# A decoder trunk on one Trainium2 core: down products in pairs of 256 columns, with their weights in two long places

## The chip, the cores and the metric

The kernel runs on one core of a Trainium2 chip. The engines are PE (TensorE, matmuls), PEld (its weight loads), ACT (ScalarE), DVE (VectorE), POOL (GpSimd) and SP (which issues DMAs). The metric is device time of one execution in microseconds (us), lower is better; "before" and "after" are two programs that compute the same.

## The reference

Two layers, each an FFN, a token mixer (differential attention in the first layer, a pooling mixer in the second), cross-attention into 256 memory tokens and another FFN, over 512 tokens of width 1024. What the change touches is the FFN, which runs four times:

```python
def swiglu_ffn(x, w_in, w_out):
    h = x @ w_in
    g, u = jnp.split(h, 2, axis=-1)
    return (jax.nn.silu(g) * u) @ w_out
...
x = layer_norm(a * x + 0.5 * swiglu_ffn(x, ffn_w_in[i, 0], ffn_w_out[i, 0]),
               ln_g[i, 0], ln_b[i, 0])
...
x = layer_norm(a * x + h, ln_g[i, 1], ln_b[i, 1])
x = layer_norm(a * x + memory_cross_attention(x, mem, xa_wq[i], xa_wkv[i], xa_wo[i]),
               ln_g[i, 2], ln_b[i, 2])
x = layer_norm(a * x + 0.5 * swiglu_ffn(x, ffn_w_in[i, 1], ffn_w_out[i, 1]),
               ln_g[i, 3], ln_b[i, 3])
```

`w_in` is 1024 x 5632, `w_out` 2816 x 1024, all in float32.

## The kernel before

**Split operands.** Each float32 operand is kept as two tiles: hi, a cast that ACT makes (`split`, or L746 in `up`), and lo, what the cast lost, a subtraction on DVE (L144, L748). `mm3` (L225) makes a product of two such operands with three matmuls, hi by hi (L231), hi by lo (L232) and lo by hi (L233).

**The FFN.** It is made of blocks of 256 hidden columns, 11 of them. `up` computes gate and value of one block and needs 7 products in place of 8, from sums of quarter matrices; each product is 24 matmuls of 256 columns, with a quarter of `w_in` as the stationary operand (`wh`, `wl`) and x or a sum of its quarters as the moving one (`xh`, `xl`, `xe`). The quarters come as `ra` and `rc`, loaded by SP and added to by POOL's accumulating DMAs (L737, L741). `down` multiplies a pair of blocks by `w_out` with 7 products too; from one split weight each makes 12 matmuls of 512 columns: for two halves of the rows (b = 0, 1) and two hidden blocks (k = 0, 1), three each. Here the hidden block (`ha`, `hb`, from `seven`) is stationary and the split weight (`wh`, `wl`) moves. The raw weights `b1` to `b4` are added to between products (L919), and the sums in PSUM are added to the tokens `X` by DVE (L935). The last three blocks go through `plain_down`, with sums `ps`.

**The order.** `FFN_TURNS` gives five turns: three ups; then two ups and a down (pairs 0 and 1), and so on, so there are four downs in an FFN. The loop of `ffn` steps through the turn's generators ("lanes") in turn, one product each: up, up, down. PE runs the matmuls in that order. ACT and DVE run what the steps issue in an order that the scheduler derives from the same order.

**Places.** A split operand of a stage comes from `hl`, which rotates over four slots of `wh` and four of `wl` (`ffn_pools`, the 4 of `stage_pools`). Pads (`to_w`, `to_x`) set where pools begin: with `APART` of 64 bytes, `ROUND` of 512 and `LINE` of 480, w tiles of an FFN lie at addresses that leave 32 when divided by 512, and x tiles (`xh`, `xl`, `xe`) at addresses that leave 480, 64 bytes below. A matmul of an up thus has its moving operand at 480 and the stationary one that follows at 32; one of a down has its moving operand at 32 like a w, and `ha` or `hb` at 480 like an x. `_x` among the bufs of `ffn_phase` is such a pad.

Of the kernel before, what the change touches and what calls it, by code (L numbers as in the profile page):

```python
# [10 lines left out]
F32R = mybir.dt.float32r  # L11
# [6 lines left out]
P = 128  # L18
D = 1024
S = 512  # L20
# [26 lines left out]
    turn=(1.0, 1.0, 1.2, 1.5),  # L47
# [21 lines left out]
APART, ROUND, LINE = {"ffn": 64, "da": 448, "pool": 64}, 512, 480  # L69
# [47 lines left out]
def drain(units):  # L117
    for _ in units:
        pass


def few(units, n):
    for _ in range(n):
        next(units, None)


class Trunk:
# [147 lines left out]
        if gate == 1:  # L275
            self.queue_behind(self.passes[2], low)

    def hl(self, shape):
        return (
            self.stage["wh"].tile(shape, F32R, tag="wh", name="wh", bufs=self.w_bufs),  # L280
            self.stage["wl"].tile(shape, F32R, tag="wl", name="wl", bufs=self.w_bufs),
        )

    def cols(self, raw, j):

        w = self.hl([P, 8, P])
        self.split_weights(w[0], w[1], raw[:, :, j * P : (j + 1) * P])
        return w
# [281 lines left out]
    def ffn(self, layer, j, ln, beside=()):  # L570
        w_in, w_out = self.a["ffn_w_in"][layer, j], self.a["ffn_w_out"][layer, j]
        self.seven_of, self.factors = {}, self.factor_tiles()
        nc, n, beside = self.nc, len(FFN_TURNS), iter(beside)
        at_start = bool(self.load_rest)
        downs = {i: self.down(d, w_out, 2.0 * ALPHA if i == 1 else 1.0) for i, (_, d) in enumerate(FFN_TURNS) if d}

        def start(turn):
            ups = FFN_TURNS[turn][0]

            early = (2, 1, 1) if turn == 0 else (0, 0)  # L580
            rest = self.load_rest.pop if turn == 0 and at_start else lambda: lambda: None
            got = [self.up(w_in, u, lane, early[lane], rest() if lane == 0 else None) for lane, u in enumerate(ups)]
            for lane, g in enumerate(got):
                next(g)
                if lane == 1:
                    rest()()
            if turn > 1:
                next(downs[turn])
            return got + [downs[i] for i in downs if i == turn]

        works = start(0)
        if at_start:

            zeros = self.act("hb", (P, P + S), mybir.dt.bfloat16)
            nc.vector.memset(zeros, 0.0)
            idle = self.aux("idle", "yz")
            self.warm(zeros, idle, 7)
            for tag, half in (("px", 0), ("py", 1)):
                for t in self.late[:2]:
                    self.turn(t, half, tag)  # L600
                if half == 0:
                    with self.tc.issue_after(self.last_turn.ins):
                        self.warm(zeros, idle, 9)
                next(works[0])
                if half == 0:
                    next(works[0])
            next(works[1])
        else:
            for w in works + works[:1]:
                next(w)  # L610
            self.turn_late(2)
        self.late = []
        next(works[0])
        act, dve = self.first_split
        if self.begins:

            for late, first in zip(self.begins, (act, dve)):
                self.queue_behind(late, first)
        second = self.second_factors()
        if at_start:  # L620

            next(works[0])
            for w in (works[1], second, second, works[1], works[2], works[2], works[0]):
                with self.behind():
                    next(w)
        else:
            for w in (second, *works[1:], second, downs[1]):
                next(w)
        for turn in range(n):
            behind = turn == n - 1  # L630
            for step in range(1 if turn == 0 else 0, 9 if behind else 7):
                if turn == 0 and (step == 3 or step == 2 and at_start):
                    next(second)
                if step == 4:
                    if behind:
                        coming = [self.plain_down(w_out, layer, j, ln, beside)]
                    else:
                        coming = start(turn + 1)
                        if at_start and turn == 0:
                            with self.tc.issue_after(self.last_load.ins):  # L640
                                next(downs[1])
                if behind and step in (4, 6, 7, 8):
                    next(coming[0])
                if behind and step > 3:
                    few(beside, 2)

                for lane, w in enumerate(works[: None if not behind or step > 1 else -1]):
                    if not (at_start and turn == 0 and lane < 2 and step == 1):
                        next(w, None)
                    if turn == 0 and lane == 1 and step == 2 and at_start:  # L650
                        next(works[0])
                    if turn == 0 and lane == 0 and step == 2 and not at_start:
                        next(second)
                    if at_start and turn == 0 and lane == 0 and step == 3:
                        next(works[2])
                if turn == 1 and step == 3:
                    self.seven_of[self.waiting[0]] = self.seven(self.waiting[1])
            works = coming
        drain(works[0])
# [236 lines left out]
    def down(self, pairs, w, scale):  # L896
# [14 lines left out]
        hs = [self.seven_of[u] for u in pairs]  # L911

        def operand(raw):
            t = self.hl([P, 2, S])
            self.split(t[0], t[1], raw)
            return [(t[0][:, i], t[1][:, i]) for i in range(2)]

# [3 lines left out]
        def product(ps, b, a, ws, start=False):  # L921

            o = slice(b * P, (b + 1) * P)
            for k in range(2):
                h, l = hs[k][a]
                self.mm3(ps, (h[:, o], l[:, o]), ws[k], start and k == 0, k == 1, not start)

        started = set()

# [6 lines left out]

        B = range(2)
        ws = operand(b11)
        more(b11, b12)
        xs = []  # L940
        for b in B:
            xs.append(self.aux("px", "px"))
            product(xs[b], b, 0, ws, True)
            add(xs[b], b, 0)
        yield
        ws = operand(b21)
        for b in B:
            ps = self.aux("py", "py")
            product(ps, b, 1, ws, True)
            add(ps, b, 0)  # L950
        yield
        ws = operand(b11)
        more(b11, b22)
        more(b12, b22)
        zs = []
        for b in B:
            zs.append(self.aux("pz", "py"))
            product(zs[b], b, 3, ws, True)
            add(zs[b], 2 + b, 1)
        yield  # L960
        ws = operand(b22)
# [4 lines left out]
        ws = operand(b11)  # L966
# [5 lines left out]
        ws = operand(b12)  # L972
# [4 lines left out]
        ws = operand(b11)  # L977
# [5 lines left out]
    def plain_down(self, w, layer, j, ln, beside):  # L983
# [8 lines left out]
        ws = [[], []]  # L992

        def operand(half, k):
            t = tiles[half][k]
            if half == 0:
                v = self.hl([P, 2, S])
            elif k < 2:
                v = self.pair("hb", (P, 2, S))
            else:  # L1000
                v = [[self.act("ha") for c in range(2)] for _ in range(2)]
                for c in range(2):
                    self.split(v[0][c], v[1][c], t[:, c])
                ws[half].append(v)
                return
            self.second = self.split(v[0], v[1], t)[1]
            ws[half].append([[x[:, c] for c in range(2)] for x in v])

        def product(ps, half, t, k, n=slice(0, S)):
            o = slice(t * P, (t + 1) * P)  # L1010
            for c in range(2):
                h = [x[:, c, o] for x in self.seven_of[FFN_LAST[k]]]
                self.mm3(ps, h, [x[c][:, n] for x in ws[half][k]], k == c == 0, k == 2 and c == 1)

        operand(0, 0)
        yield

        sums = []
        for n, (half, t) in enumerate(LAST):
# [14 lines left out]
            ps = self.aux("ps", ("yz", "py")[n % 2])  # L1034
# [691 lines left out]

    def ffn_pools(self):
        self.apart = APART["ffn"]
        return self.stage_pools(4, dict(ra=4, rc=3), ("wh", "wl", "ra", "rc"))

    def other_pools(self, order=("wh", "wl", "raw"), raw=2):
        return self.stage_pools(5, dict(raw=raw), order)

    def ffn_phase(self, **more):
        bufs = dict(b1=1, b3=1, b2=1, b4=1, _x=0, xe=6, hb=4, sp=4, ha=4, sr=1, hr=3)
        return self.phase_pool(("hr", "sr"), "sp", **bufs, **more)

    def ffn_first(self, layer, ln):
        with self.ffn_pools():
# [83 lines left out]
```

## Time and profile before

| | us |
|---|---|
| median of three runs | 1898.41 (1897.36 to 1905.37) |
| profiled execution | 1899.25 |
| its span | 1897.5 |
| PE idle for a semaphore, all waits | 3.3 |

Rows of the trace read: start in us, duration, engine, line, operation, output from inputs by the program's names, shapes, and in brackets the idle time before it and what ended it. Grouped rows end in the count, the busy time, and the mean of one in ns. Matmuls are pipelined: their durations overlap, and what one costs is the distance from its start to the next start.

### The profile page before, as it was taken

What the parts mean: (1) busy time and instruction counts of PE and PEld (TensorE: products, weight loads), DVE (VectorE), ACT (ScalarE), POOL (GpSimd) and SP (SyncE); (2) the same over time, 40 slices, a digit from 0 to 9 for tenths busy, and PEclk for the clock granted to TensorE, in tenths of its full rate; (3) what the DMA queues carried; (4) which work ended last, traced back from release to release, by engine and by line L of the source; (5) the groups of instructions that cost most, each with busy time, mean ns of one, the idle gap of its engine ahead of it and who ended that gap; (6) DMA issues with size and microseconds to landing.
All of it is one profiled execution on the core that took longest, in us unless ns stands there. A gap on an engine that the chain in (4) does not pass through costs nothing.

```text
span 1897.5 us, 32589 instructions
## 1 busy us (share of the span) xinstructions
PE 1886.5 (99%) x13120; PEld 1730.9 (91%) x13120; DVE 1540.9 (81%) x2246; ACT 1000.8 (53%) x1542; POOL 308.2 (16%) x274
## 2 busy tenths in 40 slices
PE   9999999999999999999999999999999999999998
PEld 8999998888889988999998999999899889999996
DVE  7888989888876558889887988898786568998886
ACT  6555554566654435555554655555455436555552
POOL 3112120112110002221220311212120012211210
PEclk9999999999999999999999999999999999999999
DMA  9978772322235327987785687777464438867861
GB/s 254 215 178 178 171 141 85 103 69 75 91 112 178 112 70 181 195 177 168 144 188 168 118 179 181 168 166 162 157 172 146 142 69 180 173 159 178 185 129 53
DMA packets 250055, 283.20 MB, mean 149 GB/s; under 512 B 8752, under 2 KB 213040, under 8 KB 249904
## 3 DMA queue, kind: packets, MB, share of 16 engines
q0 software_dynamic: 94080, 94.38, 32.3%
q1 hardware_dynamic: 155824, 186.74, 30.2%
q8 instruction: 103, 1.69, 0.4%
q14 instruction: 48, 0.39, 0.1%
HBM read 274.79 MB, written 4.19 MB: 147 GB/s over the span
## 4 chain that ended last, share of the span: by engine, by line
PE 96%; DMA 2%; DVE 1%; ACT 0%; SPq 0%; issue 0%; POOL 0%; DVEq 0%; ACTq 0%
PE x L231 7%; PE x L232 7%; PE x L233 7%; PE ps L231 5%; PE ps L233 4%; PE ps L232 4%; PE z L231 4%; PE z L233 4%; PE z L232 4%; PE px L233 3%; PE px L231 3%; PE px L232 3%; PE x L773 3%; PE y L231 2%; PE y L232 2%; PE y L233 2%
## 5 line engine op out<-in xcount | busy, mean ns | idle before, releaser
L741 POOL DMA_DIRECT2D ra<-in_ffn_w_in_dram x132 | 170.7, 1307 | 977.6 <-DVE wl L748 960.4
L746 ACT CAST wh<-ra 128x1024 fp32r<-128x1024 f32 x176 | 184.9, 1053 | 197.8 <-PE x L232 63.8
L748 DVE TENSOR_TENSOR wl<-ra,wh 128x1024 fp32r<-128x1024 f32 x176 | 214.2, 1220 | 64.7 <-ACT wh L746 64.0
L231 PE MATMUL x<-xe,wh 128*128 128x256 f32 x704 | 195.0, 277 | 0.0
L232 PE MATMUL x<-xe,wh 128*128 128x256 f32 x704 | 194.8, 277 | 0.0
L233 PE MATMUL x<-xe,wl 128*128 128x256 f32 x704 | 194.8, 277 | 0.0
L746 ACT CAST wh<-rc 128x1024 fp32r<-128x1024 f32 x132 | 138.9, 1053 | 100.3 <-PE x L232 41.6
L143 ACT CAST wh<-b 128x1024 fp32r<-128x1024 f32 x112 | 117.8, 1052 | 134.8 <-PE x L232 62.2
L748 DVE TENSOR_TENSOR wl<-rc,wh 128x1024 fp32r<-128x1024 f32 x132 | 159.5, 1218 | 24.7 <-ACT wh L746 24.7
L144 DVE TENSOR_TENSOR wl<-b,wh 128x1024 fp32r<-128x1024 f32 x112 | 136.7, 1220 | 40.9 <-ACT wh L143 40.9
L231 PE MATMUL x<-xh,wh 128*128 128x256 f32 x536 | 148.7, 277 | 0.0
L232 PE MATMUL x<-xl,wh 128*128 128x256 f32 x536 | 148.4, 277 | 0.0
L233 PE MATMUL x<-xh,wl 128*128 128x256 f32 x536 | 148.4, 277 | 0.0
L231 PEld LDWEIGHTS x<-xe,wh 128*128 128x128 f32 x704 | 132.4, 188 | 1.3
L232 PEld LDWEIGHTS x<-xe,wh 128*128 128x128 f32 x704 | 132.3, 188 | 1.3
L233 PEld LDWEIGHTS x<-xe,wl 128*128 128x128 f32 x704 | 132.2, 188 | 0.0
L144 DVE TENSOR_TENSOR wl<-raw,wh 128x1024 fp32r<-128x1024 f32 x64 | 78.5, 1233 | 45.8 <-ACT wh L143 45.2
L231 PEld LDWEIGHTS x<-xh,wh 128*128 128x128 f32 x536 | 100.8, 188 | 0.7
L232 PEld LDWEIGHTS x<-xl,wh 128*128 128x128 f32 x536 | 100.8, 188 | 0.7
L233 PEld LDWEIGHTS x<-xh,wl 128*128 128x128 f32 x536 | 100.7, 188 | 0.0
L143 ACT CAST wh<-raw 128x1024 fp32r<-128x1024 f32 x64 | 66.4, 1049 | 62.5 <-PE xq L232 18.2
L231 PE MATMUL z<-xe,wh 128*128 128x256 f32 x352 | 97.5, 277 | 0.0
(445 smaller groups left out, 6239.9 us busy)
## 6 DMA issues: line engine op xcount, KB each, us to landing
ra<-in_ffn_w_in_dram POOLq DMA_DIRECT2D x132, 512.0 KB, 7.0
rc<-in_ffn_w_in_dram SPq DMA_DIRECT2D x88, 512.0 KB, 5.8
b<-in_ffn_w_out_dram SPq DMA_DIRECT2D x76, 512.0 KB, 5.0
ra<-in_ffn_w_in_dram SPq DMA_DIRECT2D x44, 512.0 KB, 4.7
rc<-in_ffn_w_in_dram POOLq DMA_DIRECT2D x44, 512.0 KB, 7.3
raw<-in_xa_wkv_dram SPq DMA_DIRECT2D x16, 1024.0 KB, 5.4
raw<-in_da_w_qkv_dram SPq DMA_DIRECT2D x24, 512.0 KB, 3.7
raw<-in_xa_wq_dram SPq DMA_DIRECT2D x8, 1024.0 KB, 5.2
```

What stands on the lines that cost most here:

```text
L143: self.nc.scalar.copy(hi, src),
L144: self.nc.vector.tensor_sub(lo, src, hi.bitcast(F32)),
L231: self.first_mm = mm(out, w[0], x[0], start=start, stop=False, skip_group_check=again)
L232: mm(out, w[0], x[1], start=False, stop=False, skip_group_check=again)
L233: self.last_mm = mm(out, w[1], x[0], start=False, stop=stop, skip_group_check=again)
L741: nc.gpsimd.dma_start(t, source(*block), accum_op=ALU.add)
L746: hi = nc.scalar.copy(v[0], raw)
L748: lo = nc.vector.tensor_sub(v[1], raw, v[0].bitcast(F32))
L773: self.last_mm = nc.tensor.matmul(ps[:, j], v[i][:, k, j * P : (j + 1) * P], x[l][:, k], start=n == i == l == 0, stop=n == 7 and i == 1, s ...
```

## The change

`down` now computes each half's product in two parts of 256 columns: for columns 0 to 255 and then 256 to 511, the same 12 matmuls, so a product that was 12 matmuls of 512 columns is 24 of 256. Its split weights come no longer from `hl` but alternate between two long places, `above` (beside `wh` and `wl`, in the stage's pools) and `below` (among the phase's tiles, in place of the pad). A long place holds hi and lo behind each other, and has room for an offset, which puts the operand where x tiles lie (480) or where w tiles lie (32). For the downs it is as x, while `ha` and `hb` move to where w tiles lie, since the pad before them is gone.

`wh` and `wl` have two slots each instead of four. In turn 0, and in step 0 of turn 1, `hl` rotates by fours: two operands to the long places, two to `wh` and `wl`. Five operands get the place of what they meet, by the flag `alike`: one of turn 0, step 4, in each of the four FFNs, and one of a down in turn 1, step 2, of the first. `plain_down` uses the long places as x and gives `hb` an offset; its step at turn 4, step 6 comes behind the second lane instead of ahead of the lanes. The gains of the layer norm are kept in `hr` twice, instead of `hr` and `sr`.

```diff
-    def hl(self, shape):
+    def hl(self, shape, down=None):
+        if down is None and "below" in self.bufs:
+            self.slot += self.by_fours
+            if self.by_fours and self.slot % 4 < 2:
+                alike, self.alike = self.alike, False
+                return self.long_place(self.slot % 2, shape, alike)
...
+    def long_place(self, below, shape, as_x):
+        n, near, far = 2 * S, self.apart // 4, (ROUND - self.apart) // 4
+        if below:
+            t, at = self.act("below", (P, 2 * n + near)), 0 if as_x else near
+        else:
+            t = self.stage["above"].tile([P, 2 * n + far], F32R, tag="above", name="above", bufs=1)
+            at = far if as_x else 0
+        return tuple(t[:, at + i : at + i + n].rearrange("p (a b) -> p a b", a=shape[1]) for i in (0, n))
...
+        self.slot, self.by_fours, self.alike = 0, True, False
...
-                if behind and step in (4, 6, 7, 8):
+                if behind and step in (4, 7, 8):
                     next(coming[0])
...
+                self.by_fours = turn == 0 or turn == 1 and step == 0
+                self.alike = turn == 0 and step == 4 or at_start and turn == 1 and step == 2
                 for lane, w in enumerate(works[: None if not behind or step > 1 else -1]):
...
+                    if behind and step == 6 and lane == 1:
+                        next(coming[0])
...
         def operand(raw):
-            t = self.hl([P, 2, S])
+            self.slot += 1
+            t = self.long_place(self.slot % 2, (P, 2, S), not self.alike)
...
-            for k in range(2):
-                h, l = hs[k][a]
-                self.mm3(ps, (h[:, o], l[:, o]), ws[k], start and k == 0, k == 1, not start)
+            for c, e in ((0, 2 * P), (2 * P, S)):
+                for k in range(2):
+                    h, l = hs[k][a]
+                    self.mm3(
+                        ps[:, c:e], (h[:, o], l[:, o]), [w[:, c:e] for w in ws[k]],
+                        start and c == k == 0, k == 1 and e == S, True,
+                    )
...
             if half == 0:
-                v = self.hl([P, 2, S])
+                self.slot += 1
+                v = self.long_place(self.slot % 2, (P, 2, S), True) if k else self.hl([P, 2, S], True)
             elif k < 2:
-                v = self.pair("hb", (P, 2, S))
+                far = (ROUND - self.apart) // 4
+                v = [t[:, far : far + 2 * S].rearrange("p (a b) -> p a b", a=2) for t in self.pair("hb", (P, far + 2 * S))]
...
-        return self.stage_pools(4, dict(ra=4, rc=3), ("wh", "wl", "ra", "rc"))
+        return self.stage_pools(2, dict(ra=4, rc=3), ("wh", "wl", "above", "ra", "rc"))
...
-        bufs = dict(b1=1, b3=1, b2=1, b4=1, _x=0, xe=6, hb=4, sp=4, ha=4, sr=1, hr=3)
-        return self.phase_pool(("hr", "sr"), "sp", **bufs, **more)
+        bufs = dict(b1=1, b3=1, b2=1, b4=1, sr=1, xe=6, below=1, hb=4, sp=4, ha=4, hr=3)
+        return self.phase_pool(("hr", "hr"), "sp", **bufs, **more)
```

How the order of the instructions moves is shown at three places, each of before (line numbers of before) and then of after (its own line numbers). The first is PE at the first down product of the first FFN; `px` is its sum in PSUM, `ha` the hidden block, `x` and `y` sums of the ups beside it. Before, its 12 matmuls end like this:

```order
L233 MATMUL x<-xh,wl 128x256
L231 MATMUL px<-wh,ha 128x512
L232 MATMUL px<-wl,ha 128x512
L233 MATMUL px<-wh,ha 128x512
L231 MATMUL px<-wh,ha 128x512
```

After, the same place:

```order
L233 MATMUL x<-xh,wl 128x256
L231 MATMUL px<-above,ha 128x256
L232 MATMUL px<-above,ha 128x256
L233 MATMUL px<-above,ha 128x256
L231 MATMUL px<-above,ha 128x256
```

Four such groups of three stood there, and eight stand there now, with half the columns and hi and lo both in `above`.

The second is DVE in the first FFN, where the fourth turn begins, around the adds of its down's first product to the tokens (`X_76`, `X_77`, by `px`) and the subtraction that makes the lo part of that down's second operand (from `b`, into `wl` before and a long place after). Before:

```order
L935 SCALAR_TENSOR_TENSOR X_76<-X_76,px 128x512
L888 TENSOR_TENSOR sr<-hr 128x256
L891 TENSOR_TENSOR sr<-hr 128x256
L889 SCALAR_TENSOR_TENSOR sr<-sr,hr 128x256
L935 SCALAR_TENSOR_TENSOR X_77<-X_77,px 128x512
L890 SCALAR_TENSOR_TENSOR sr<-sr,hr 128x256
L824 TENSOR_TENSOR hr<-y,sp 128x2x256
L144 TENSOR_TENSOR wl<-b_1957,wh 128x1024
L748 TENSOR_TENSOR wl<-ra,wh 128x1024
```

After:

```order
L144 TENSOR_TENSOR below<-b_2069,below 128x1024
L912 SCALAR_TENSOR_TENSOR sr<-sr,hr 128x256
L144 TENSOR_TENSOR hb<-hr,hb 128x256
L770 TENSOR_TENSOR wl<-rc,wh 128x1024
L144 TENSOR_TENSOR hb<-sr,hb 128x1024
L962 SCALAR_TENSOR_TENSOR X_76<-X_76,px 128x512
L910 TENSOR_TENSOR sr<-hr 128x256
L913 TENSOR_TENSOR sr<-hr 128x256
L911 SCALAR_TENSOR_TENSOR sr<-sr,hr 128x256
L962 SCALAR_TENSOR_TENSOR X_77<-X_77,px 128x512
```

The subtraction for that operand (`b_1957` before, `b_2069` after) stood behind the two adds to `X` by `px`, and stands ahead of them now.

The third is ACT at the end of cross-attention and the start of the second FFN. `oT` is attention's output, `p` and `var` belong to the layer norm, `xh` is the normed x, turned (`pt`) and cast, and `ra` and `rc` are quarters of `w_in`. Before:

```order
L143 CAST oT<-xo 128x512 x3
L746 CAST wh<-ra 128x1024 x3
L397 ACTIVATE p,var<-X_76,mean 128x1024
L746 CAST wh<-rc 128x1024
L398 ACTIVATE var<-var 128x1
L397 ACTIVATE p,var<-X_77,mean 128x1024
L398 ACTIVATE var<-var 128x1
L143 CAST xh<-pt 128x4x128 x2
L397 ACTIVATE p,var<-X_78,mean 128x1024
L143 CAST xh<-pt 128x4x128
```

After:

```order
L143 CAST oT<-xo 128x512 x3
L768 CAST above<-rc 128x1024
L768 CAST wh<-ra 128x1024 x2
L414 ACTIVATE p,var<-X_76,mean 128x1024
L415 ACTIVATE var<-var 128x1
L414 ACTIVATE p,var<-X_77,mean 128x1024
L415 ACTIVATE var<-var 128x1
L143 CAST xh<-pt 128x4x128 x2
L414 ACTIVATE p,var<-X_78,mean 128x1024
L143 CAST xh<-pt 128x4x128
L415 ACTIVATE var<-var 128x1
L143 CAST xh<-pt 128x4x128
```

Three casts of `ra` and one of `rc` stood ahead of the first cast of `xh`. Now one of `rc` and two of `ra` do, and the next row behind the last one shown is `CAST below<-ra`, the first operand that PE needs in this FFN. On PE the first product of the FFN used to be 24 matmuls of that one operand, and then `pt` for the third quarter of the tokens; now 16 of them, 15 of another lane's product and the other 8 come ahead of that `pt`.

## The prediction

> **What bounds the kernel now.** I read the page first: the busy shares, the granted clock in 40 slices, and the chain that ended last.
>
> ```profile
> PE 1886.5 (99%) x13120; PEld 1730.9 (91%) x13120; DVE 1540.9 (81%) x2246; ACT 1000.8 (53%) x1542; POOL 308.2 (16%) x274
> ...
> PEclk9999999999999999999999999999999999999999
> ...
> PE 96%; DMA 2%; DVE 1%; ACT 0%; SPq 0%; issue 0%; POOL 0%; DVEq 0%; ACTq 0%
> ```
>
> TensorE is busy for 99% of the span, it is 96% of the last chain, and its clock is full in every slice. So time can only come from two places: gaps on PE, or the start-to-start time of a matmul. The waits of PE (line waited for and releaser; total us, times, longest us) show how little the gaps hold:
>
> ```profile
> PE idle L138 <- DVE hb L595: 1.3, 1, 1.3
> PE ps L231 <- DVE X L380: 0.8, 1, 0.8
> PE y L773 <- ACT wh L746: 0.5, 1, 0.5
> PE xq L233 <- DVE wl L144: 0.3, 1, 0.3
> PE po L1247 <- DVE a L144: 0.2, 1, 0.2
> PE pt L515 <- DVE X L403: 0.2, 1, 0.2
> ```
>
> 3.3 us in all. What is left is the time of one matmul, and that has to be read from starts: the durations in the rows (0.28 us for 256 columns) overlap, since matmuls are pipelined. Next the timeline of PE around one down product, and the windows (length; busy time and count by engine; clock; DMA share; GB/s) of three stretches without a wait:
>
> ```profile
> 109.73 0.39 PE L231 MATMUL px<-wh,hb 128*128 128x512 f32 x1
> ...
> 112.48 0.28 PE L231 MATMUL x<-xe,wh 128*128 128x256 f32 x1
> ...
> 117.94 0.39 PE L231 MATMUL px<-wh,hb 128*128 128x512 f32 x1
> ```
>
> ```profile
> 34.54:76.83 42.29, 42.29 (x361) 42.29 (x360) 33.24 (x39) 24.37 (x31) 10.31 (x8) 1.00 1.16 250
> 745.31:799.60 54.29, 54.29 (x482) 54.29 (x480) 47.30 (x54) 34.63 (x45) 14.21 (x11) 1.00 0.92 175
> 109.73:241.14 131.41, 131.41 (x962) 123.55 (x961) 115.00 (x144) 69.45 (x83) 21.91 (x18) 1.00 0.74 171
> ```
>
> The counts include two or three matmuls that only overlap an edge; what starts inside is 359, 479 and 960. The second window is a turn with only 256-column matmuls: 54.29/479 = **113.3 ns** each. The third holds 16 cycles of one down product (12 matmuls of 512 columns) and two up products (48 of 256): 131.41/16 = 8.213 us a cycle. Of one cycle the timeline shows 12 matmuls in 112.48 − 109.73 = 2.75 us, 229 ns each where two of 256 take 226.7, and 48 in 5.46 us where 48 × 113.3 ns = 5.44: the 512s cost some 30 ns a product, and the 256s behind them some 20 ns until they are back at 113.3. The first window is the other finding: 256-column matmuls at 42.29/359 = **117.8 ns**, 4.46 ns more, at the same clock of 1.00 and with no wait on the list. It begins behind a matmul of 34.32 us that took twice the usual step, and it ends at the first 512:
>
> ```profile
> 34.32 0.38 PE L773 MATMUL z<-xh,wh 128*128 128x256 f32 x1
> 34.54 0.28 PE L773 MATMUL z<-xl,wh 128*128 128x256 f32 x1
> ...
> 76.71 0.28 PE L233 MATMUL x<-xh,wl 128*128 128x256 f32 x1
> 76.83 0.40 PE L231 MATMUL px<-wh,ha 128*128 128x512 f32 x1
> ```
>
> So a stream of 256s has two paces, a short one of 113.3 and a long one of 117.8 ns, and keeps the one it has.
>
> **The change part by part.** *Pairs of 256 columns.* The groups of PE by shape give the number of down matmuls; L232 and L233 have the same counts:
>
> ```profile
> L231 PE MATMUL px<-wh,hb 128*128 128x512 f32 x192 | 75.1, 391 | 0.1
> L231 PE MATMUL pz<-wh,hb 128*128 128x512 f32 x128 | 49.7, 388 | 0.0
> L231 PE MATMUL px<-wh,ha 128*128 128x512 f32 x64 | 24.9, 389 | 0.0
> L231 PE MATMUL py<-wh,ha 128*128 128x512 f32 x64 | 24.9, 388 | 0.0
> ```
>
> 448 × 3 = 1344 matmuls, 112 blocks of 12. They become 2688 of 256 columns, whose moving operand now lies to the stationary one as x lies to w in the up products, so I give them the same 113.3 ns. A cycle is then 72 × 113.3 ns = 8.160 us instead of 8.213: 0.053 us less, and 112 × 0.053 = **−5.9 us**. The bounds: at 117.8 ns the halves cost 24 × 4.46 ns = 0.107 us a block more than that, so +6.0 us instead of −5.9; no row is below 113.3. I take 113.3, the pace of the turn before the downs begin.
>
> A rule of the Trainium skill speaks against this term: its page "TensorE: Matmul & The Clock Gate", section "Back-to-back issue gap", gives an isolated gap of the columns over 2.4 GHz plus a fixed 2.5 ns for each matmul, so cutting one in two should cost 2.5 ns: 1344 × 2.5 = 3.4 us more, an estimate from that page. The windows here disagree: two of 256 take 226.7 ns and one of 512 takes 229.
>
> *The stretch at the long pace in the first FFN.* In it the z product of turn 0, step 4, comes 190 matmuls behind 34.54 and gets an operand placed alike with x; the 145 from there on ran at the long pace. What a block of equal placement does to the pace, the trace shows only with 512s, at the end of the plain down:
>
> ```profile
> 1058.28 0.39 PE L231 MATMUL ps<-ha,xe 128*128 128x512 f32 x1
> 1058.51 0.39 PE L232 MATMUL ps<-ha,xe 128*128 128x512 f32 x1
> 1058.73 0.39 PE L233 MATMUL ps<-ha,xe 128*128 128x512 f32 x1
> 1058.96 0.28 PE L773 MATMUL x<-xh,wh 128*128 128x256 f32 x1
> ...
> 1060.84 1.11 PE L773 MATMUL x<-xh,wl 128*128 128x256 f32 x8
> 1061.79 0.49 PE L515 MATMUL pt<-ident,X 128*128 128x128 f32 x3
> ```
>
> Those three take 0.68 us, 226.7 ns each; but the 24 matmuls behind them (16 single ones and the group of 8) take 2.83 us, 117.9 ns each. So an equal block is itself at full pace and may leave the long pace behind it. Bounds for this term: −1.6 us if all 359 run at the short pace (359 × 4.46 ns), 0 if nothing changes, and worse as a rival below. I take the short pace behind the block, as the 512s of other placement left it at 76.83: 145 × 4.46 ns = **−0.65 us**. The borders of the five alike blocks cost at most what a border of a 512 block costs (20 to 30 ns, twice each): **+0.2 us**.
>
> *Two slots for split weights and two long places instead of four slots.* Now ACT and DVE must still be ahead of PE:
>
> ```profile
> 219.45 1.05 ACT L746 CAST wh<-rc 128x1024 fp32r<-128x1024 f32 x1 [1.81 <-PE pz L233]
> 222.08 1.05 ACT L746 CAST wh<-rc 128x1024 fp32r<-128x1024 f32 x1 [1.58 <-PE x L232]
> ```
>
> ```profile
> 198.59 1.21 DVE L144 TENSOR_TENSOR wl<-b,wh 128x1024 fp32r<-128x1024 f32 x1
> ```
>
> ```profile
> 200.30 0.39 PE L232 MATMUL py<-wl,ha 128*128 128x512 f32 x1
> ```
>
> ACT's cast starts when PE leaves the slot, which was four products back: three products, 8.2 us, ahead of its use. With two slots for the ups alone there are one up and one down between release and use: 2 × 2.72 = 5.4 us, less the cast's 1.05 and the subtraction's 1.21, so some 3 us are left for what stands ahead on DVE. The tightest row now is the py operand: its subtraction ends at 199.80, and PE reads wl at 200.30, 0.50 us later. In the new order that subtraction stands several rows earlier, as its place was freed by the last down but one, five products ahead. So 0 us; if the cover is gone PE waits, priced below.
>
> *The start of the second FFN.* The first operand now goes to `below`, in the order behind all four xh<-pt casts on ACT, because cross-attention still uses that memory:
>
> ```profile
> 715.34 1.05 ACT L746 CAST wh<-ra 128x1024 fp32r<-128x1024 f32 x1 [6.40 <-DMA ra<-in_ffn_w_in_dram]
> ...
> 733.64 0.57 ACT L143 CAST xh<-pt 128x512 fp32r<-128x512 f32 x1
> ```
>
> ```profile
> 718.32 0.50 PE L231 MATMUL ps<-kv,oT 128*128 128x512 f32 x1 [0.81 <-DVE X L380]
> ...
> 734.25 0.28 PE L773 MATMUL x<-xh,wh 128*128 128x256 f32 x1
> ...
> 737.49 1.07 PE L515 MATMUL pt<-ident,X 128*128 128x128 f32 x8 [0.18 <-DVE X L403]
> ```
>
> The last of those casts ends at 734.21, the operand's own at 734.21 + 1.05 = 735.3, while PE wants it at 734.25: up to +1.05 us, and pt, X adds and all later work queue behind it. Against that, 15 more matmuls (1.7 us) now stand ahead of pt, so its wait of 0.18 goes, and the cast at 715.34 with its subtraction, which kept DVE from the add that PE waited 0.81 us for, is now rc's, and earlier. 1.05 − 0.99 = 0.06: I take 0, with −1.0 and +1.5 as ends. The third and fourth FFN use the same places behind the plain down and the mixer; no PE wait is there now, and I add no cost.
>
> *The rest.* At turn 4, step 6, one cast and one subtraction move behind two products; no DMA moves with them, and what needs them starts one step later. Gains of the norm in another buffer, and the offset of `hb`, move no instruction on PE: 0 us, at best −0.4 where the plain down's 512s reach 226.7.
>
> **Sum.** 1899.25 (the profiled execution) − 5.9 − 0.65 + 0.2 = 1892.9. The median of the runs, 1898.41, is 0.84 below that execution: **1892.1 us**, −0.33%. A measurement of this kernel can tell about 0.5%, 9.5 us, from no change.
>
> **The rivals.**
> 1. *The long pace stays (slower than before).* In the kernel before, a 512 block ended it after 359 matmuls; after the change no 512 stands inside the turns of an FFN, and a stream that leaves an alike block or a wait at the long pace may stay so to its end. An FFN has 11 × 7 × 24 up and 4 × 7 × 24 = 672 down matmuls, 2520, of which some 2400 run behind its start-up: 2400 × 4.46 ns = 10.7 us. For it: the 359 at 117.8 ns, and the 24 behind an equal block. Against it: 479 in a row at 113.3. In one FFN: 1892.1 + 10.7 = 1902.8, still within 0.5%; with two, 1913.5; with all four, 1935. It decides from the second such FFN on.
> 2. *The pair buys nothing.* The new halves run at 114.5 (half of 229) to 117.8 ns: from 1898 to 1904. Against it: the pace of the up products with the same offset. The rule of the skill named above would be inside this.
> 3. *PE is starved.* Half a microsecond (the 0.50 us of slack, turned around) at each of the 16 turns with a down: +8, so 1900. Against it: 3 us of slack by the rows.
>
> **How the numbers follow.** Forecast 0.60; the long pace in one FFN 0.17, in more than one 0.13; the pair buys nothing 0.05; starved 0.05. Faster by over 0.5% (below 1888.9) needs every term at its good end: 1892.1 − 0.95 (all 359 at the short pace) − 1.0 − 0.4 = 1889.8, and the scatter of the runs, 1 us below their median: 0.12 out of the forecast. Slower by over 0.5% (above 1907.9): the 0.13 and a little of the others, 0.15. The rest, 0.73, is within. The range from 1887 to 1904 holds the forecast with its ends, one FFN at the long pace and most of rivals 2 and 3, and leaves out several such FFNs.
>
> **What would show it.** Right: px to px in steady turns at 8.16 us; 256s of the downs at 113.3 ns; behind the alike block of the first FFN 113.3 ns; PE's waits still some 3 us. Wrong: a window of an FFN without waits at 117.8 ns per matmul (rival 1), or only the downs' matmuls above 113.3 (rival 2), or waits of PE for wh, above or below in the turns (rival 3).

## The result, and the profile after

| | us |
|---|---|
| median after, 4 runs | 1926.24 (1925.73 to 1926.56) |
| median before, 4 runs | 1898.72 (1897.36 to 1905.37) |
| ratio after to before | 1.0137 (95% interval 1.0117 to 1.0157) |
| profiled execution after, its span | 1926.16, 1924.4 |

The change makes the kernel slower by 1.4%. The forecast was 1892.1, and the range ended at 1904; for three FFNs at the long pace rival 1 gives 1892.1 + 3 × 10.7 = 1924.2. The page of the changed kernel, in the parts shown of before (busy time by engine, granted clock in 40 slices, the chain that ended last):

```profile
PE 1910.7 (99%) x14464; PEld 1809.5 (94%) x14464; DVE 1553.2 (81%) x2246; ACT 1000.2 (52%) x1542; POOL 306.6 (16%) x274
...
PEclk9999999999999999999999999999999999999999
...
PE 93%; DVE 4%; DMA 1%; ACT 1%; issue 1%; POOL 0%; SPq 0%; DVEq 0%; ACTq 0%; POOLq 0%
```

The 1344 matmuls that were added are there, and PE is as busy as before at the same clock: the page alone doesn't tell where 27 us went. Its waits (line waited for and releaser; total us, times, longest us) hold 2.6 us more than before, 5.9 in place of 3.3:

```profile
PE x L795 <- ACT below L768: 2.3, 2, 1.5
PE px L231 <- DVE X L962: 1.4, 1, 1.4
PE idle L138 <- DVE hb L613: 1.3, 1, 1.3
PE ps L232 <- DVE wl L144: 0.3, 1, 0.3
PE pt L532 <- DMA X<-in_x_dram: 0.2, 1, 0.2
PE ps L232 <- DVE above L144: 0.2, 1, 0.2
PE po L1276 <- DVE a L144: 0.2, 1, 0.2
```

The rest is the pace, which is read from starts. Four windows of the changed kernel (length; busy time and count by engine; clock; DMA share; GB/s): three steady cycles of the first FFN, the second FFN from its first full pace to the fourth step, from there to the last matmul of its turns, and three steady cycles in between:

```profile
110.47:134.95 24.48, 24.48 (x218) 24.48 (x217) 23.44 (x31) 13.39 (x17) 2.59 (x2) 1.00 0.60 154
747.63:771.54 23.91, 23.91 (x213) 23.91 (x212) 23.42 (x25) 18.15 (x24) 9.67 (x8) 1.00 0.77 130
771.54:1025.99 254.45, 254.45 (x2162) 254.45 (x2161) 217.35 (x264) 132.11 (x160) 43.13 (x34) 1.00 0.75 161
836.61:862.05 25.44, 25.44 (x219) 25.44 (x217) 23.87 (x31) 13.39 (x17) 2.59 (x2) 1.00 0.59 153
```

Of the counts two or three only overlap an edge: 216, 211, 2160 and 216 start inside. In the first FFN a cycle takes 24.48/3 = 8.16 us, the forecast to the last digit: all 72 matmuls at 113.3 ns. In the second the same cycle takes 25.44/3 = 8.48 us, 117.8 ns each, and so does all of it from 771.54 on, while the 211 matmuls ahead ran at 23.91/211 = 113.3. The pace turns over at one matmul. The timeline of PE there:

```profile
771.32 0.28 PE L232 MATMUL z<-xe,above 128*128 128x256 f32 x1
771.43 0.28 PE L233 MATMUL z<-xe,above 128*128 128x256 f32 x1
771.54 0.28 PE L231 MATMUL x<-xe,below 128*128 128x256 f32 x1
771.66 0.28 PE L232 MATMUL x<-xe,below 128*128 128x256 f32 x1
771.78 0.28 PE L233 MATMUL x<-xe,below 128*128 128x256 f32 x1
771.90 0.28 PE L231 MATMUL x<-xe,below 128*128 128x256 f32 x1
```

Steps of 0.11 to 0.12 us up to 771.54, of 0.12 from it. `x<-xe,below` is the equal block of turn 0, step 4. An equal block is a product of 24 matmuls whose two operands have the same place, both at 480 or both at 32 by the kernel's pads; here the weights are placed as the moving operand. (The prediction called it a z product, 190 matmuls into the first FFN's stretch; it is the x product behind z, 96 matmuls into it.) The third and fourth FFN do the same: 211 matmuls at 113.3 ns ahead of their block and 2184 at 117.8 from it on. The first FFN goes long at its own block too, at 45.88 us, and comes back 432 matmuls later, at the end of the second equal block that only it has, the down product `pz`:

```profile
96.49 0.28 PE L231 MATMUL pz<-above,hb 128*128 128x256 f32 x1
96.61 0.28 PE L232 MATMUL pz<-above,hb 128*128 128x256 f32 x1
96.73 0.28 PE L233 MATMUL pz<-above,hb 128*128 128x256 f32 x1
96.85 0.29 PE L231 MATMUL z<-xe,wh 128*128 128x256 f32 x1
96.97 0.28 PE L232 MATMUL z<-xe,wh 128*128 128x256 f32 x1
97.09 0.28 PE L233 MATMUL z<-xe,wl 128*128 128x256 f32 x1
97.21 0.28 PE L231 MATMUL z<-xe,wh 128*128 128x256 f32 x1
```

Behind 97.09 the steps are back at 113.3 ns (the window from 110.47 above). So the sum against the profiled execution of before: three FFNs with 24 + 2160 long matmuls, 3 × 2184 × 4.46 ns = 29.2 us; the first FFN 432 long ones where before had 359, 0.3; the pairs −5.9; PE's waits 2.6. Together 26.2 of the 26.9 us between 1899.25 and 1926.16.

### The profile page after: what moved, and what is told of

Read it like the earlier page. It is cut to its first block, busy times and chain, and to the rows that moved or that the text cites. A ratio compares the mean times of both kernels' runs of the same rounds, so it can differ in the third digit from the quotient of the medians.

```text
span 1924.4 us, 35092 instructions
## 1 busy us (share of the span) xinstructions
PE 1910.7 (99%) x14464; PEld 1809.5 (94%) x14464; DVE 1553.2 (81%) x2246; ACT 1000.2 (52%) x1542; POOL 306.6 (16%) x274
## 4 chain that ended last, share of the span: by engine, by line
PE 93%; DVE 4%; DMA 1%; ACT 1%; issue 1%; POOL 0%; SPq 0%; DVEq 0%; ACTq 0%; POOLq 0%
PE x L232 7%; PE x L231 7%; PE x L233 7%; PE z L232 4%; PE z L231 4%; PE z L233 4%; PE ps L231 4%; PE ps L232 4%; PE ps L233 4%; PE x L795 3%; PE px L232 3%; PE px L231 3%; PE px L233 3%; PE y L232 2%; PE y L231 2%; PE y L233 2%
## 5 line engine op out<-in xcount | busy, mean ns | idle before, releaser
L768 ACT CAST wh<-ra 128x1024 fp32r<-128x1024 f32 x152 | 159.6, 1050 | 205.8 <-PE x L232 105.8
L770 DVE TENSOR_TENSOR wl<-ra,wh 128x1024 fp32r<-128x1024 f32 x152 | 185.3, 1221 | 42.0 <-ACT wh L768 40.9
L770 DVE TENSOR_TENSOR wl<-rc,wh 128x1024 fp32r<-128x1024 f32 x112 | 136.8, 1222 | 54.7 <-ACT wh L768 54.4
L768 ACT CAST wh<-rc 128x1024 fp32r<-128x1024 f32 x112 | 117.6, 1050 | 119.9 <-PE x L232 75.3
L231 PE MATMUL x<-xe,wh 128*128 128x256 f32 x608 | 170.2, 280 | 0.0
L232 PE MATMUL x<-xe,wh 128*128 128x256 f32 x608 | 170.2, 280 | 0.0
L233 PE MATMUL x<-xe,wl 128*128 128x256 f32 x608 | 170.2, 280 | 0.0
L231 PEld LDWEIGHTS x<-xe,wh 128*128 128x128 f32 x608 | 116.2, 191 | 0.0
L233 PEld LDWEIGHTS x<-xe,wl 128*128 128x128 f32 x608 | 114.1, 188 | 0.0
L232 PEld LDWEIGHTS x<-xe,wh 128*128 128x128 f32 x608 | 114.1, 188 | 0.0
L143 ACT CAST above<-b 128x1024 fp32r<-128x1024 f32 x60 | 63.1, 1051 | 50.1 <-PE pz L233 26.2
L231 PE MATMUL z<-xe,wh 128*128 128x256 f32 x312 | 87.1, 279 | 0.0
L232 PE MATMUL z<-xe,wh 128*128 128x256 f32 x312 | 87.1, 279 | 0.0
```

Of the source, the lines that this page charges most:

```text
L143: self.nc.scalar.copy(hi, src),
L231: self.first_mm = mm(out, w[0], x[0], start=start, stop=False, skip_group_check=again)
L232: mm(out, w[0], x[1], start=False, stop=False, skip_group_check=again)
L233: self.last_mm = mm(out, w[1], x[0], start=False, stop=stop, skip_group_check=again)
L768: hi = nc.scalar.copy(v[0], raw)
L770: lo = nc.vector.tensor_sub(v[1], raw, v[0].bitcast(F32))
```

## The experiments

Each was timed beside the kernel before on the same chip, whose medians were 1898.3 to 1899.1. Edits are against the changed kernel where nothing else is said. Three theories stood: A, an equal block turns the pace over; B, an equal block of the first kind (both at 480) sets the long pace and one of the second (both at 32) the short one, whatever came before; C, the blocks have nothing to do with it.

**No equal block.**

```diff
-                self.alike = turn == 0 and step == 4 or at_start and turn == 1 and step == 2
+                self.alike = False
```

> The changed kernel with no operand placed alike, all else as it is. Theory A (an equal block turns the pace over, from 113.3 to 117.8 ns a matmul and back): the three later FFNs run at 113.3 ns from turn 0 to the plain down, 3 x 2184 x 4.46 ns = 29.2 us less, and the first FFN some 450 matmuls more, 2.0 us less: 1926.2 - 31 = 1895 us. Theory B (an equal block with both at 480 leaves 117.8 ns behind it, one with both at 32 leaves 113.3): the same, 1895. Theory C (the long pace comes from the long places themselves or from the waits at the start of an FFN, not from the equal blocks): 1926 as before, with 117.8 ns from the same place on.

Measured: median 1905.15 us of 10 runs, ratio 1.0027 (1.0004 to 1.0050), and a scatter that the changed kernel doesn't have and the kernel before has only in single runs (four of its five sets have one at 1905.4 to 1906.6): four runs from 1895.66 to 1897.78, five from 1904.87 to 1907.95, one at 1916.74. Only the first four are near the 1895 that theories A and B gave. The groups lie some 10 us apart, about one FFN at the long pace (10.7 by the forecast's estimate). So the blocks cause what the changed kernel shows, and theory C falls; but without them the pace of an FFN is open. In the profiled run (the one at 1916.74) the second FFN is long from its beginning to its end:

```profile
754.05:1036.72 282.67, 282.67 (x2402) 282.67 (x2400) 243.29 (x291) 153.17 (x188) 52.78 (x41) 1.00 0.76 157
```

2400 matmuls in 282.67 us, 117.8 ns each, behind waits at the FFN's start; the first is long too, and the third and fourth are short but for the fourth's last 357. The long pace needs no equal block, and nothing inside the turns ends it.

**An equal block of the second kind in each FFN, none of the first.**

```diff
+                self.alike = turn == 1 and step == 2
```

> The changed kernel with an equal block only in the down of turn 1, step 2 (both at 32), but in all four FFNs, none in turn 0. Theory A: each FFN comes to it at 113.3 ns and leaves it at 117.8: 1895 + 4 x 1751 x 4.46 ns = 1895 + 31 = 1926 us, with the long pace from the z product behind that block. Theory B: it leaves 113.3 ns: 1895 us. Theory C: the long pace stands ahead of the block already.

Measured: 1898.07 us of 10 runs (1895.24 to 1902.18), ratio 0.9999 (0.9990 to 1.0008). Theory B, and A falls: the block leaves the short pace though it is reached at the short one. Two windows of the second FFN, ahead of the block and behind it, up to a short delay in the last turn:

```profile
745.65:799.49 53.84, 53.84 (x478) 53.84 (x476) 47.84 (x59) 35.50 (x47) 14.26 (x11) 1.00 0.92 176
819.03:976.93 157.90, 157.90 (x1395) 157.90 (x1394) 141.27 (x175) 85.22 (x103) 27.15 (x22) 1.00 0.79 171
```

475 and 1392 matmuls (less the edges), 113.4 ns each.

**Two equal blocks of the first kind in turn 0, none of the second.**

```diff
+                self.alike = turn == 0 and step in (4, 6)
```

> The changed kernel with two equal blocks of the same kind (both at 480) in turn 0 of each FFN, 168 matmuls from one to the next, and none in turn 1. Theory A: the second turns the pace back: 1895 + 4 x 168 x 4.46 ns = 1898 us, 117.8 ns between the two blocks only. Theory B: 117.8 ns from the first to the plain down in all four FFNs: 1895 + 4 x 2160 x 4.46 ns = 1895 + 38.5 = 1934 us.

Measured: 1934.22 us (1933.12 to 1936.31), ratio 1.0189 (1.0174 to 1.0204), theory B's 1934. Two windows of the third FFN, ahead of the first block and from it on:

```profile
1089.43:1113.34 23.91, 23.91 (x213) 23.91 (x212) 22.14 (x23) 15.45 (x20) 10.43 (x9) 1.00 0.80 131
1113.34:1370.67 257.33, 257.33 (x2186) 257.33 (x2185) 219.06 (x266) 134.33 (x163) 42.45 (x33) 1.00 0.75 160
```

Here and in the fourth FFN, 211 and some 210 matmuls run at 113.3 ns up to the first block, and 2184 at 117.8 from it on; the second block changes nothing. The first and second FFN were long ahead of their first block already, behind waits, and stay so. The second kind of block is missing, and no FFN comes back.

**The second kind added to the changed kernel's first.**

```diff
+                self.alike = turn == 0 and step == 4 or turn == 1 and step == 2
```

> The changed kernel with one thing added: the second equal block (a down's, both at 32, turn 1, step 2), which the first FFN has, in the three later FFNs too. Theory B: each FFN runs at 117.8 ns from the first block to the second, 409 matmuls or 1.8 us, and at 113.3 behind it: 1895.2 + 4 x 1.8 = 1902.5 us, with little scatter, since both blocks set the pace. If the second block only helped in the first FFN, 1926.

Measured: 1906.92 us of 5 runs (1905.63 to 1907.91), ratio 1.0039 (1.0025 to 1.0053): 19 us below the changed kernel, 4 above what was expected. The pace goes long at the first block and short at the second in all four FFNs; in the second FFN, between the blocks and behind the second one:

```profile
771.69:822.66 50.97, 50.97 (x434) 50.97 (x433) 44.90 (x59) 29.09 (x37) 8.56 (x8) 1.00 0.85 178
823.02:1021.27 198.25, 198.25 (x1752) 198.25 (x1750) 171.94 (x207) 105.63 (x126) 34.21 (x27) 1.00 0.77 162
```

432 matmuls take 118.0 ns each, 1749 take 113.4. The 4 us are in the last turn, where three of the four go long again for 357 matmuls (3 × 1.6 us). It happens at this place of PE's timeline, the third FFN's first z product of the last turn, whose third matmul starts 0.12 us and whose fourth 0.12 to 0.13 us behind the one ahead:

```profile
1305.59 0.28 PE L231 MATMUL z<-xh,wh 128*128 128x256 f32 x1
1305.70 0.28 PE L232 MATMUL z<-xl,wh 128*128 128x256 f32 x1
1305.82 0.29 PE L233 MATMUL z<-xh,wl 128*128 128x256 f32 x1
1305.94 0.28 PE L231 MATMUL z<-xh,wh 128*128 128x256 f32 x1
```

The subtraction that makes this `wl` on DVE:

```profile
1304.45 1.21 DVE L770 TENSOR_TENSOR wl<-ra,wh 128x1024 fp32r<-128x1024 f32 x1
```

It ends at 1305.66, 0.16 us ahead of its use. PE loses some 0.02 us, too little for the list of waits, and its pace may change with this hiccup. Read over all traces, the size of the delay goes with what is left behind: the hiccup was met at this place and at the short pace 31 times. The 12 times in which it took 243 to 248 ns from the second matmul's start to the fourth's left the long pace, the 19 with 249 to 257 left the short one; without a delay it is 2 × 113.3 = 226.7. No run varied this delay by itself, so that its size decides isn't shown.

**The pair without the places.** The kernel before, with the pairs of `down` and nothing else:

```diff
-            for k in range(2):
-                h, l = hs[k][a]
-                self.mm3(ps, (h[:, o], l[:, o]), ws[k], start and k == 0, k == 1, not start)
+            for c, e in ((0, 2 * P), (2 * P, S)):
+                for k in range(2):
...
```

> The kernel before with the down products in pairs of 256 columns and nothing else: split weights in the four slots, moving at 32 against a stationary operand at 480. If the pair alone is what pays, the downs' matmuls take 113.3 ns and the time is 1898.7 - 5.9 = 1893, if the first FFN stays at the short pace behind its turn 0, or up to 8 more if it keeps the long one. If the placement is what pays, they take more than half of 229 ns, 114.5 to 117.8, with a border on each side: 1898 to 1907.

Measured: 1914.12 us (1912.54 to 1915.83), ratio 1.0083 (1.0066 to 1.0099), outside both. The halves run at either pace, and each change from a down to the ups turns the pace over, while the change from the ups to a down keeps it. One round of four windows (a down product, the two ups behind it, the next down, 46 matmuls of the ups behind that):

```profile
108.99:111.71 2.72, 2.72 (x27) 2.72 (x25) 2.52 (x4) 2.05 (x3) 0.00 (x0) 1.00 1.08 380
111.71:117.37 5.66, 5.66 (x51) 5.66 (x50) 5.55 (x8) 2.11 (x2) 0.00 (x0) 1.00 0.66 207
117.37:120.19 2.82, 2.82 (x26) 2.82 (x25) 2.30 (x3) 1.05 (x1) 0.00 (x0) 1.00 0.80 244
120.43:125.65 5.22, 5.22 (x49) 5.22 (x47) 3.43 (x4) 2.56 (x3) 1.31 (x2) 1.00 0.40 116
```

24 in 2.72 us (113.3), 48 in 5.66 (117.9), 24 in 2.82 (117.5), 46 in 5.22 (113.5). The matmuls of the ups pay for it too, which the expectation had left out.

**The places without the pair.** 512 columns in the long places, and no equal block (`self.alike = False`):

```diff
-            for c, e in ((0, 2 * P), (2 * P, S)):
-                for k in range(2):
...
+            for k in range(2):
+                h, l = hs[k][a]
+                self.mm3(ps, (h[:, o], l[:, o]), ws[k], start and k == 0, k == 1, not start)
```

> The changed kernel with its long places but down products of 512 columns again, and no operand placed alike. If the placement as x's is what takes the borders away, a 512 block costs 2 x 113.3 ns a matmul and no border, and the time is that of the changed kernel without alike operands, from 1895 up, with scatter if a 512 no longer ends the long pace. If the 512s themselves cost the 229 ns and the border, whatever their place, the time is that of the kernel before, about 1898, without scatter, since each down sets the short pace anew.

Measured: 1906.00 us (1905.23 to 1909.44), ratio 1.0043 (1.0026 to 1.0060), a part of each. A steady down product and the 47 matmuls behind its border:

```profile
110.74:113.54 2.80, 2.80 (x15) 2.26 (x14) 2.60 (x4) 2.06 (x3) 0.00 (x0) 1.00 0.94 301
113.66:118.98 5.32, 5.32 (x49) 5.32 (x48) 5.32 (x8) 2.12 (x2) 0.00 (x0) 1.00 0.49 146
```

12 matmuls take 2.80 us, 233 ns each where they took 229; the border is gone (the 256 ahead of the second window took 0.12 us, and the next 47 took 5.32, 113.2 each), and every down still leaves the short pace. So the pair and the places need each other: the places take away the border, and the pair brings 2 × 113.3 in place of 233.

**Waits that are left.** Two blocks of the second kind, the second in the last turn:

```diff
+                self.alike = turn == 1 and step == 1 or turn == 4 and step == 4
```

> The changed kernel with equal blocks of the down's kind only (both at 32), in all four FFNs: one at turn 1, step 1, and one at turn 4, step 4. Theory B (such a block leaves 113.3 ns, whatever came before): each FFN runs long at most in its first 550 matmuls (2.5 us each, by the wait ahead) and from a late hiccup to turn 4, step 4: median 1897, all within 1894.5 to 1900, and less scatter than with one block. If the second block does harm from the short pace, it shows 117.8 ns behind it (143 matmuls, 0.6 us an FFN).

Measured: 1899.00 us of 10 runs (1896.32 to 1900.44), ratio 1.0002 (0.9993 to 1.0011). The block in the last turn does bring the short pace back (in the second FFN from 1003.41 on), but three of four FFNs had gone long at the z product shown above. Then one block (turn 1, step 2), with the rotation of the long places begun one operand later in the FFNs behind the first:

```diff
-        self.slot, self.by_fours, self.alike = 0, True, False
+        self.slot, self.by_fours, self.alike = int(not self.load_rest), True, False
```

> The kernel with one equal block of the down's kind in each FFN (turn 1, step 2), and besides the rotation of the long places begun one operand later in the three later FFNs, so that the first operand of the second FFN goes to the short slots and not to the long place that cross-attention still reads. If that wait of PE (1.2 us at the start of the second FFN, where the kernel before has none) is the long place's, it goes: 1.2 us less than the kernel with one block, 1896.9 at the median. If the casts of x are what PE waits for, nothing changes: 1898.

Measured: 1896.96 us of 10 runs (1895.23 to 1901.18), ratio 0.9993 (0.9983 to 1.0002). The wait for `below` goes from the start of the second FFN and one of 1.0 us for `pt` comes in its place; against the kernel with one block the intervals overlap, and a second timing of the same kernel, meant for the last experiment, gave 1898.86 (1895.45 to 1902.33), ratio 0.9999 (0.9990 to 1.0008):

> The same without that edit, on the same chip: median 1897, up to 1901, and of the four FFNs those with the hiccup in the last turn may run long behind it.

Two blocks, the later start, and the old step order of the plain down:

```diff
-                if behind and step in (4, 7, 8):
+                if behind and step in (4, 6, 7, 8):
...
-                    if behind and step == 6 and lane == 1:
-                        next(coming[0])
```

> Both together, and the plain down's step at turn 4, step 6 back ahead of the lanes: two blocks of the down's kind in each FFN, the later start of the long places, and the old step order, which takes away PE's wait of 1.4 us for the tokens' add at the first plain sums: 1897 - 1.2 - 1.4 = 1894.5 us at the median if all three hold; 1897 if only the blocks count.

Measured: 1898.83 us of 10 runs (1897.98 to 1900.35), ratio 0.9999 (0.9989 to 1.0008), a miss. The wait of `px`, 1.4 to 1.5 us in the first FFN's last down, goes, and one of 1.6 us for an up's `wl` in the last turn stands in its place. One block, one step earlier, and the later start:

```diff
+                self.alike = turn == 1 and step == 1
```

> The kernel with one block of the down's kind in each FFN and the later start of the long places, the block one step earlier (turn 1, step 1). If the scatter above 1895.2 us is the pace of the first 500 to 600 matmuls of each FFN, which the block ends 72 matmuls sooner, the median is 0.3 us an FFN at most below that of the block at step 2: 1896.0 to 1897.0 us, 0.1% below the kernel before. If the late hiccup in turn 4 makes the scatter, nothing changes: 1897, up to 1901.

Measured: 1898.34 us of 12 runs (1896.76 to 1901.09), ratio 0.9997 (0.9988 to 1.0006); no gain that can be told. And the kernel with one block at step 2 and the later start, with the rotation by fours in steps 0 and 1 of the last turn:

```diff
-                self.by_fours = turn == 0 or turn == 1 and step == 0
+                self.by_fours = turn == 0 or turn == 1 and step == 0 or behind and step < 2
```

> The kernel with one block of the down's kind in each FFN (turn 1, step 2) and the later start of the long places, and in steps 0 and 1 of the last turn, where two ups stand without a down between them, the rotation by fours of turn 0 again. If the late hiccup of PE (18 to 22 ns at the third matmul of the last turn's first z product) is the two short slots coming free one product too late there, it goes from all four FFNs, and with it the long pace behind it (357 matmuls, 1.6 us, where it struck): all runs within 1894.5 to 1898.5, median 1896. If it is something else, it stays and so does the scatter up to 1901.

Measured: 1897.78 us of 11 runs (1895.36 to 1900.41), ratio 0.9994 (0.9984 to 1.0003), half a miss: the z product has no hiccup any more in any of the four FFNs, where the two traces without that edit have it in all four, and in the third and fourth 1749 and 1750 matmuls in a row are short; but in the first and second it moved to a y product with a step of 0.28 us, and the second is long behind it. Of all these versions none is clear of the kernel before; with one block of the second kind they are 27 to 29 us below the changed kernel.

## Why the prediction was wrong

**The step that failed** is in the part on the stretch at the long pace: "I take the short pace behind the block, as the 512s of other placement left it at 76.83". The only rows of an equal block were the `ps` ones at 1058.28, with 24 long matmuls behind them, and the text drew from them that such a block "may leave the long pace behind it". It does so each time that the traces show: the four blocks with both at 480 in the changed kernel and the four in the kernel with the second kind added were all reached at the short pace, and all left 117.8 ns behind them. The trace of before had a second such place, which the prediction didn't read: the plain down of the third FFN ends with the same `ps<-ha,xe` matmuls, and the 87 of 256 columns behind them are long. In the changed kernel `ha` lies at 32, and the same 87 behind the same matmuls are short (before, then after; from the first start to the last, 86 steps of 117.8 and of 113.5 ns):

```profile
1381.81:1391.94 10.13, 10.13 (x87) 10.12 (x86) 9.44 (x13) 4.91 (x9) 2.81 (x3) 1.00 0.93 282
1400.53:1410.29 9.76, 9.76 (x87) 9.76 (x86) 9.07 (x14) 4.22 (x8) 2.83 (x3) 1.00 0.96 270
```

The forecast set the rows of 512s above the rows that had the block's own placement, for one stretch of 145 matmuls, and gave the three FFNs with no second block no term in the sum.

**Rival 1 was the mechanism, and its size was right:** 10.7 us an FFN was its price, 3 × 2184 × 4.46 ns = 29.2 us is what came, and it came in more than one FFN, which had 0.13. The rival named the equal block and a wait as what may leave the long pace, but took it as a chance for each FFN, where the block sets it in every one that reaches it and has nothing to set it back. The kernel without equal blocks shows that chance. In the first FFN, where the forecast had −0.65 us, 432 long matmuls in place of 359 cost 0.3.

**The pair** was worth in a cycle what the sum said, 8.16 us at the short pace, but not in a run. The profiled run of the kernel with one block of the second kind (all FFNs short) is at 1895.24, 4.0 us below the profiled run of before, where the −5.9 of the pairs and −1.6 for the first FFN make 7.5; its waits are 2.2 us longer by the list, and the rest is open. That run is also the fastest of its ten, and at the median the gain is nothing (1898.07 beside 1898.44). The bounds on the halves were right as well, since they ran at 113.3 and at 117.8, by the pace of the whole stream. Rival 2 was wrong in its form: the downs have no pace of their own in the changed kernel.

**The slots** were not free: 3 us of slack holds where a down stands between the ups, but the last turn's first two steps have two ups each and no down, and there a short slot comes free one product ahead of its use instead of two: 2.72 − 1.05 − 1.21 leaves 0.46 us, and the row of DVE ahead of the subtraction (`hr<-y,sp`, 0.68) takes more. The last experiment fits this, since the hiccup leaves the z product when its operands go to the long places. The 0.02 us that it costs on PE isn't the price; the pace behind it is, up to 357 × 4.46 ns = 1.6 us an FFN. The changed kernel itself didn't pay it: its first FFN left the hiccup at the short pace, and the other three were long already. That this turn has no down until its third step was in the order, and the walk through it left it out. **The start of the second FFN** stands in the changed kernel's timeline of PE:

```profile
734.79 0.39 PE L233 MATMUL ps<-kv,oT 128*128 128x512 f32 x1
735.97 0.39 PE L795 MATMUL x<-xh,below 128*128 128x256 f32 x1 [0.79 <-ACT below L768]
```

1.18 us from start to start, where one of these 512s takes 0.23: 0.95 us lost, near the 1.05 of the prediction; from the last down matmul of the first FFN to the first z of the second it is 449.2 us before (304.20 to 753.36) and 450.0 after (305.25 to 755.22), so 0.8 us net stayed, where the forecast took 0 and had 1.5 as its bad end. PE's waits rose by 2.6 us in all, to which the forecast gave 0. The two largest new ones stand elsewhere: 1.5 us for `below` at the start of the first FFN, which the prediction didn't weigh, and 1.4 us for `px` in its last down, behind the first plain sums, where the step moved at turn 4, step 6 had been put at 0; with the old step order that wait goes.

**The rule of the Trainium skill** that was weighed, on the page "TensorE: Matmul & The Clock Gate", section "Back-to-back issue gap", gives 256 columns one isolated gap. The runs here have two, 113.3 and 117.8 ns at a clock of 1.00, and 512 columns take 229 or 233 by their place.

**What stays open:** why a block with both operands at 480 sets the long pace and one with both at 32 the short one. The blocks differ in kind too, an up's with x moving and a down's with a hidden block standing. The `ps<-ha,xe` rows above, with a hidden block moving and x standing, speak for the place in the first case, since of this block only the place of `ha` differs; for both at 32 no run swapped the kinds. That the places are 480 and 32 is read from the kernel's pads, not from a trace. Nor did a run remove all waits at the start of an FFN, which let the pace fall either way; the later start of the long places only moved one.

## What to carry to other kernels

A stream of equal matmuls can hold two steady paces a few per cent apart for thousands of instructions, with no wait and a full clock in the profile: count starts in a window that has no wait before believing a mean. A change that takes away what set the pace anew (here the 512s) makes everything that can set it, a wait of 20 ns as well, worth the rest of the stream. Weigh a rule of placement by rows with that very placement, however few, above any number of rows with another.

## What the runs showed of the hardware

- 256-column float32r matmuls, each with its own weight load, run 113.3 or 117.8 ns apart; the pace stays, for 2400 matmuls in one run, until something changes it.
- What changes it, with the places by the kernel's pads: a block of 24 with both operands at 480 modulo 512 bytes (long, from its first matmul), a block with both at 32 (short, two or three matmuls behind it; in the block itself 119 to 120 ns), a change from offset −64 to +64 bytes and back (turned over at each way back, with pairs in the old places), a 512 block with unequal places (short; with both at 480 long, for the 24 and 87 matmuls that follow), and a wait (either; at the hiccup of the last turn long behind a delay of 16 to 21 ns and short behind 22 to 30).
- 512-column matmuls took 229 ns in the downs with the moving operand at 32 and the weights at 480, 233 the other way round, and 226.7 with both at 480.
